# A four-layer conditioned trunk in fp32: first loads reordered, operands laid out at multiples of 256 bytes, one sub-layer's end split into halves

## The chip, the cores and the metric

The kernel runs on one core of one Trainium2 chip. The time is device microseconds of one execution; the figure for the kernel before is the median of three runs.

## The reference, cut to what matters

There are 512 tokens of width 1024 and four layers. Each layer has a token mixer (layer 0 a Conformer convolution module, 1 HGRN2, 2 mLSTM, 3 stick-breaking attention) and then a causal gated convolutional FFN of inner width 2816. A vector c modulates each of the eight sub-layers.

```
m = silu(c) @ ada_w[i] + ada_b[i]          # 6 x 1024: shift, scale, gate, twice
h = x * (1 + scale) + shift
x = LayerNorm(alpha * x + (1 + gate) * f(h))
# f of layer 0:
u = glu(h @ w_pw1 + b_pw1);  u = causal_dwconv(u, width 31)
f = silu(layer_norm(u)) @ w_pw2 + b_pw2
```

## The kernel before, in words

All arithmetic is in fp32. A large matrix product is done in three products of float32r operands: each operand is split into a high part (a cast on ScalarE, ACT) and a low part (a subtraction on VectorE, DVE), and TensorE (PE) adds high·high, high·low and low·high in PSUM. Weights stream from HBM once, in units of 128 x 1024 (512 KB). `unit` (L231) loads one into a `raw` buffer (three of them) of the pool `wp`, multiplies it by the gate row where it belongs to an output projection (L242), and `parts` (L247) makes `wh` (L252) and `wl` (L254).

An input projection (`up_mm`, L277) has the weights as the stationary operand and the activations `hh`, `hl` of the pool `xp` as the moving one. An output projection (`down`, L332; `mm` at L345, matmul at L351) has the activations stationary and the weights moving: for each pair of 128 inner rows `kp`, for each block of 128 tokens `t`, six matmuls of 512 columns. `head` makes `down` go over the first pairs for tokens 0 to 255 first and then for tokens 256 to 511; `tail` (3) does the last three pairs token block by token block, so that each can be finished early; the last two of these pairs have their `wh`, `wl` in `spare` tiles of the stage's own pool.

SBUF tiles lie one behind another in pools, at multiples of 32 bytes. By the addresses of the program, `wp` and `xp` (raw, wh, wl, hh, hl, X) lie 192 bytes past a multiple of 256, the FFN's stage pool (the activations `gr..h`, `gr..l` and the spare weights) 64 bytes past one, HGRN's activations 96 or 224 bytes, those of the mLSTM's output projection and of the attention's 64 bytes, and the operands of the mLSTM's value product (`mn`) at 0. In the output projections of HGRN's values (`p_hv`), the attention's values (`p_sv`) and the Conformer (`p_pw`, L351) both operands are at 192.

The modulation is a product with one vector, done on DVE: `ada_unit` (L203) loads 512 KB of ada_w and multiplies and sums it against silu(c) laid out on all partitions (`sbc`), which gives one of 48 columns of a layer. `fill` slips such units between the units of an input projection; `flush` does what is left up to a given column. Columns 0 to 15 are needed for the first h, 16 to 23 for the gate of the mixer, 24 to 39 for the FFN's h.

All loads go out on SyncE's (SP's) queue, in order: a load that waits for a free buffer holds up those behind it. The order of instructions on each engine is worked out by a scheduler at build time, from priorities (the order of the code, weights earlier) and estimated times; then each engine is in order.

The start (`first_h`, L525): loads of the identity, c broadcast to 128 partitions, the layer's parameters, four tiles of X, and then, for each of eight blocks k, two ada units, transposes of X, hf (ACT), hh, hl, and the matmuls of the first four pw1 units.

The Conformer (L627): for each of eight channel blocks j, two pw1 units (with one and two ada units after them, L661 and L662), GLU into `upad` (L667), a spill to DRAM (`ud`, L670) and four loads back with a shift (`R`, L672), 56 convolution matmuls (`pc`, L681), the remaining taps on DVE, transposes to token-major and statistics (L653 to L657). Then LayerNorm of four token blocks (L696), transposes back (L703), SiLU (L705), the split into high and low parts (`ring`, L325 and L326), the gate (`gate_rows`, L433) and `down` with pw2.

Of the kernel before, what the change touches and what calls it, by code (L numbers as in the profile page):

```python
# [10 lines left out]
F32 = mybir.dt.float32  # L11
# [5 lines left out]
P = 128  # L17
# [31 lines left out]
HEAD = 3  # L49

# [19 lines left out]
def pack(inp):  # L70
# [3 lines left out]
    o["c"] = a["c"].reshape(1, D)  # L74
# [65 lines left out]

class Trunk:
    def __init__(self, ctx, tc, ins, out):
# [15 lines left out]
        self.mhalf = self.const.tile([P, 8], F32, name="mhalf")  # L158
# [3 lines left out]
        nc.sync.dma_start(out=cb, in_=ins["c"].broadcast_to([P, D]))  # L162
# [21 lines left out]
    def begin_layer(self, i):  # L184
# [5 lines left out]
        ab = self.sp.tile([P, 48], F32, tag="adab", name=f"adab{i}")  # L190
# [3 lines left out]
        ac = self.sp.tile([P, 48], F32, tag="adac", name=f"adac{i}")  # L194
# [286 lines left out]
    def mod_cols(self, i, which, prev):  # L481
# [10 lines left out]
        GB = self.sp.tile([P, 2 * KD], F32, tag="GB", name=f"GB{i}_{which}")  # L492
# [32 lines left out]
    def first_h(self, i, w=None, us=(), name=None):  # L525
# [5 lines left out]
        with tc.tile_pool(name="start", bufs=1, side="right", reuse_waits="tile") as st:  # L531
# [19 lines left out]
    def sub_end(self, ep, i, which, nxt, bias=None, gate=None, due=True):  # L551
# [22 lines left out]
        def evict(h, t, ps, partial=False):  # L574
# [7 lines left out]
            if h == 0:  # L582
                st[t] = self.sp.tile([P, 2, 6], F32, tag="st", bufs=4, name=f"st_{name}_{t}")
# [22 lines left out]
    def rstd(self, st, name):  # L606
        nc = self.nc
        mv = self.sp.tile([P, 4], F32, tag="mv", bufs=4, name=f"mv_{name}")
# [18 lines left out]
    def conformer(self, nxt):  # L627
# [9 lines left out]
        with tc.tile_pool(name="cf", bufs=1, reuse_waits="tile") as op, ExitStack() as es, \  # L637
                tc.tile_pool(name="cd", bufs=1, space=bass.MemoryType.DRAM) as dr:
# [4 lines left out]
            cf = es.enter_context(tc.tile_pool(name="cg", bufs=1, reuse_waits="tile"))  # L643
# [47 lines left out]
            self.flush(i, 40)  # L691
# [689 lines left out]
```

## Time and profile before

| | us |
|---|---|
| median of 3 runs (2715.63 to 2717.45) | 2715.64 |
| the profiled execution | 2719.89 |
| its span | 2718.1 |
| PE, DVE, ACT busy in it | 2620.6, 1991.0, 1192.1 |

A busy PE is not PE at its peak: matmuls overlap, and the mean duration of one says less than the distance from one start to the next. Where a window of the timeline is full of one kind of matmul, its length divided by their number gives that distance; the count in a window takes in the matmuls that reach in from outside, which is 1 to 2 of them at 0.39 us each. In the trace a plain fp32 matmul stands as two.

### The profile page before, as it was taken

Reading aid. Unit: us, or ns where it says so; the run is one execution under the profiler, and the core shown is the slowest. Engines: PE = TensorE matmul, PEld = TensorE weight load, DVE = VectorE, ACT = ScalarE, POOL = GpSimd, SP = SyncE. Lnnn points to the kernel's source line nnn. Section 1 sums busy time; section 2 is a strip of 40 time slices with the busy share of each in tenths; the row PEclk is TensorE's granted clock in tenths of the full one; section 3 lists DMA queues with packets and bytes.
Section 4 is the critical chain, followed back from the end, with each engine's and each line's share of the span. In section 5 each row is a group of like instructions: output and inputs, shape, how many; then the busy total and the mean of one; then the engine's idle time right before and its main releaser. Section 6 shows DMA issues by size and latency. Waiting matters only on the chain.

```text
span 2718.1 us, 33772 instructions
## 1 busy us (share of the span) xinstructions
PE 2620.6 (96%) x13012; PEld 2099.0 (77%) x13012; DVE 1991.0 (73%) x3051; ACT 1192.1 (44%) x1750; POOL 43.3 (2%) x80
## 2 busy tenths in 40 slices
PE   7979999999998999999999999999999999999998
PEld 5537888887876788888887778888887776888886
DVE  7558997775677799666766777898676577766676
ACT  3124433334774443334555543543434454543332
POOL 0000000000000000000000000000000000000000
PEclk9989999999998999999999999999999999999999
DMA  8843874232221386223222223675323311323232
GB/s 318 242 115 129 299 246 155 97 115 90 86 67 51 114 300 229 93 97 107 87 90 73 86 78 116 211 266 167 101 93 98 96 55 47 101 94 116 93 97 74
DMA packets 109529, 352.66 MB, mean 130 GB/s; under 512 B 12088, under 2 KB 22328, under 8 KB 109368
## 3 DMA queue, kind: packets, MB, share of 16 engines
q1 hardware_dynamic: 109368, 350.50, 39.2%
q8 instruction: 102, 1.67, 0.2%
q14 instruction: 59, 0.48, 0.1%
HBM read 341.96 MB, written 8.50 MB: 129 GB/s over the span
## 4 chain that ended last, share of the span: by engine, by line
PE 81%; DVE 8%; ACT 5%; DMA 3%; issue 2%; POOL 1%; SPq 0%; POOLq 0%; DVEq 0%; ACTq 0%
PE p_f L282 35%; PE p_d L351 16%; PE p_mup L282 6%; PE p_mdn L351 3%; PE p_hqf L282 2%; PE p_sqk L282 2%; PE p_pw L282 2%; PE p_hv L351 1%; PE p_sv L351 1%; PE p_pw L351 1%; DMA ada<-in_ada_dram 1%; PE ms L981 1%; ACT hf L515 1%; PE p_hg L282 1%; DMA r_swo<-in_swo_dram 1%
## 5 line engine op out<-in xcount | busy, mean ns | idle before, releaser
L282 PE MATMUL p_f<-hl,wh_f 128*128 128x512 f32 (+1 forms) x1504 | 565.4, 376 | 1.2 <-DVE hl L522 1.2
L282 PE MATMUL p_f<-hh,wl_f 128*128 128x512 f32 (+1 forms) x1504 | 564.8, 376 | 0.0
L282 PE MATMUL p_f<-hh,wh_f 128*128 128x512 f32 (+1 forms) x1504 | 564.1, 376 | 0.0
L252 ACT CAST wh_f<-r_f 128x1024 fp32r<-128x1024 f32 x176 | 185.0, 1052 | 340.8 <-PE p_f L282 308.3
L282 PEld LDWEIGHTS p_f<-hl,wh_f 128*128 128x128 f32 x1504 | 283.1, 188 | 53.0 <-DVE hl L522 1.6
L282 PEld LDWEIGHTS p_f<-hh,wh_f 128*128 128x128 f32 x1504 | 282.6, 188 | 52.2 <-ACT hh L521 0.9
L282 PEld LDWEIGHTS p_f<-hh,wl_f 128*128 128x128 f32 x1504 | 283.0, 188 | 51.0 <-issue 0.2
L254 DVE TENSOR_TENSOR wl_f<-r_f,wh_f 128x1024 fp32r<-128x1024 f32 x176 | 214.9, 1223 | 136.3 <-ACT wh_f L252 135.8
L208 DVE CUSTOM_DVE_ANT_0 ada<-ada,sbc,adab 128x1024 f32<-128x1024 f32 x192 | 243.4, 1278 | 8.3 <-DMA ada<-in_ada_dram 8.3
L1312 DVE SCALAR_TENSOR_TENSOR cv<-p_f,par,cv 128x511 f32<-128x511 f32 (+1 forms) x176 | 131.1, 745 | 1.4
L1312 DVE SCALAR_TENSOR_TENSOR cg<-p_f,par,cg 128x511 f32<-128x511 f32 (+1 forms) x176 | 131.1, 745 | 1.3
L242 DVE TENSOR_TENSOR r_d<-r_d,gate 128x1024 f32<-128x1024 f32 x88 | 107.5, 1222 | 27.7 <-DMA r_d<-in_fdn_dram 26.7
L1322 ACT ACTIVATE cg<-cg 128x512 f32<-128x512 f32 x88 | 55.4, 629 | 162.2 <-DVE cg L1312 162.2
L254 DVE TENSOR_TENSOR wl_d<-r_d,wh_d 128x1024 fp32r<-128x1024 f32 x88 | 107.4, 1221 | 11.3 <-ACT wh_d L252 11.3
L282 PE MATMUL p_mup<-hh,wh_mup 128*128 128x512 f32 (+1 forms) x280 | 108.4, 387 | 0.9 <-ACT hf L515 0.9
L282 PE MATMUL p_mup<-hh,wl_mup 128*128 128x512 f32 (+1 forms) x280 | 107.1, 382 | 0.0
L282 PE MATMUL p_mup<-hl,wh_mup 128*128 128x512 f32 (+1 forms) x280 | 106.6, 381 | 0.0
L252 ACT CAST wh_d<-r_d 128x1024 fp32r<-128x1024 f32 x88 | 92.3, 1048 | 20.0 <-PE p_f L282 16.0
L624 ACT ACTIVATE X<-X,mv 128x512 f32<-128x512 f32 x56 | 43.1, 810 | 82.0 <-DVE mv L612 82.0
L1310 ACT ACTIVATE cg<-p_f,par 128x512 f32<-128x512 f32 x88 | 68.1, 774 | 13.8 <-PE p_f L282 13.8
L351 PE MATMUL p_d<-wl_d,gr0h 128*128 128x512 f32 x176 | 69.6, 396 | 0.0
L351 PE MATMUL p_d<-wl_d,gr2h 128*128 128x512 f32 x176 | 69.6, 396 | 0.0
(469 smaller groups left out, 5619.5 us busy)
## 6 DMA issues: line engine op xcount, KB each, us to landing
ada<-in_ada_dram SPq DMA_DIRECT2D x192, 512.0 KB, 4.8
r_f<-in_fup_dram SPq DMA_DIRECT2D x176, 512.0 KB, 3.7
r_d<-in_fdn_dram SPq DMA_DIRECT2D x88, 512.0 KB, 3.3
r_mup<-in_mup_dram SPq DMA_DIRECT2D x32, 512.0 KB, 3.3
r_pw<-in_pw_dram SPq DMA_DIRECT2D x24, 512.0 KB, 6.9
r_hqf<-in_hqf_dram SPq DMA_DIRECT2D x16, 512.0 KB, 3.3
r_mdn<-in_mdn_dram SPq DMA_DIRECT2D x16, 512.0 KB, 3.3
r_sqk<-in_sqk_dram SPq DMA_DIRECT2D x16, 512.0 KB, 3.6
```

The source lines that it names most:

```text
L208: nc.vector.tensor_tensor_reduce(out=raw, in0=raw, in1=self.sbc, scale=1.0, scalar=ab[:, j:j + 1], op0=ALU.mult, op1=ALU.add, accum_out=ac ...
L242: nc.vector.tensor_tensor(out=r, in0=r, in1=gr, op=ALU.mult)
L252: nc.scalar.copy(hi, raw)
L254: nc.vector.tensor_tensor(out=lo, in0=raw, in1=hi.bitcast(F32), op=ALU.subtract)
L282: self.nc.tensor.matmul(ps[:, c0:c1], a, b[:, k, c0:c1], start=(n == 0), stop=(n == 3 * KD - 1))
L351: self.nc.tensor.matmul(bank, l[:, ts_], r, start=(kp == first and a == n == 0), stop=(kp == last and a == 1 and n == 2))
L515: nc.scalar.activation(out=hf[:, j, :], in_=ps[:, j * P:(j + 1) * P], func=AF.Identity, scale=G[:, k:k + 1], bias=B[:, k:k + 1])
L624: nc.scalar.activation(out=o[:, hs], in_=x[:, hs], func=AF.Identity, scale=mv[:, 2:3], bias=mv[:, 3:4])
L981: nc.tensor.matmul(ps[:, :n], a[:, c + sb * P:c + (sb + 1) * P], b[:, c + sb * P:c + T], start=(q == 0 and k == 0), stop=(q == 3 and k == 2))
L1310: nc.scalar.activation(out=o, in_=ps, func=AF.Identity, scale=w[2], bias=par[:, C_CONVB + m:C_CONVB + m + 1])
L1312: nc.vector.scalar_tensor_tensor(out=o[:, s:], in0=ps[:, :T - s], scalar=w[2 - s], in1=o[:, s:], op0=ALU.mult, op1=ALU.add)
L1322: nc.scalar.activation(out=cg, in_=cg, func=AF.Silu)
```

## The change

- All pools but three small ones round each tile up to a multiple of 256 bytes (class `Lines`, method `pool`). Small tiles (st, mv, GB, adab, adac, ones, mhalf, and some of HGRN's and mLSTM's) move to pools of their own (`few`, `sm`, `hs`, `mk`) and to one tile at the right edge, sized so that all other tiles start at multiples of 256 bytes.
- c comes from the host already laid out on 128 rows. The order of the first loads becomes c, parameters, two ada units, identity, X. 32 matmuls of ones (into a transpose bank, read by nothing) stand ahead of the first transposes.
- In the Conformer, two ada units instead of three per channel block; the gate is made ahead of the LayerNorm; LayerNorm, transposes, SiLU and the split go in two halves of 256 tokens, the cast of every second block on DVE; the last eight ada units follow the halves; `down` gets head = 3.

```diff
@@ constants
+LINE = 256
+BUSY = 32
@@ pack
-    o["c"] = a["c"].reshape(1, D)
+    o["c"] = np.tile(a["c"].reshape(1, D), (P, 1))
@@ new
+class Lines:
+    def __init__(self, pool):
+        self.pool = pool
+
+    def tile(self, shape, dtype, **kw):
+        n = int(np.prod(shape[1:]))
+        w = LINE // 4
+        if n % w == 0:
+            return self.pool.tile(shape, dtype, **kw)
+        t = self.pool.tile([shape[0], (n + w - 1) // w * w], dtype, **kw)[:, 0:n]
...
@@ Trunk.__init__
-        self.const = E(tc.tile_pool(name="const", bufs=1))
-        self.wp = E(tc.tile_pool(name="wp", bufs=2))
-        self.xp = E(tc.tile_pool(name="xp", bufs=1))
-        self.sp = E(tc.tile_pool(name="sp", bufs=2))
-        self.ps = E(tc.tile_pool(name="ps", bufs=1, space=PSUM))
+        few = E(tc.tile_pool(name="few", bufs=1))
+        few.tile([P, 16], F32, name="edge_l")
+        self.edge = E(tc.tile_pool(name="edge", bufs=1, side="right")).tile([P, 56], F32, name="edge_r")
+        self.const = E(self.pool(name="const", bufs=1))
+        self.wp = E(self.pool(name="wp", bufs=2))
+        self.xp = E(self.pool(name="xp", bufs=1))
+        self.sp = E(self.pool(name="sp", bufs=2))
+        self.sm = E(tc.tile_pool(name="sm", bufs=2))
+        self.ps = E(self.pool(name="ps", bufs=1, space=PSUM))
...
-        nc.sync.dma_start(out=self.ident, in_=ins["ident"])
-        self.ones = self.const.tile([P, 1], F32, name="ones")
+        self.ones = few.tile([P, 1], F32, name="ones")
...
-        nc.sync.dma_start(out=cb, in_=ins["c"].broadcast_to([P, D]))
+        nc.sync.dma_start(out=cb, in_=ins["c"])
+    @contextmanager
+    def pool(self, **kw):
+        with self.tc.tile_pool(**kw) as p:
+            yield p if "space" in kw else Lines(p)
     def load_x(self):
+        self.nc.sync.dma_start(out=self.ident, in_=self.ins["ident"])
         for t in range(NT):
@@ first_h
+        nc.vector.tensor_copy(self.hh[:, KD - 1, :], self.ones.broadcast_to([P, T]))
+        ps = self.trbank("busy")
+        for n in range(BUSY):
+            nc.tensor.matmul(ps, self.onesr, self.hh[:, KD - 1, :], start=True, stop=True)
...
             hl = []
+            self.ada_unit(st, 8)
+            self.ada_unit(st, 8)
+            self.load_x()
             for u in us:
                 self.pre[u] = self.bank(f"p_{name}_{u}")
             for k in range(KD):
-                self.ada_unit(st, 8)
-                self.ada_unit(st, 8)
+                if k:
+                    self.ada_unit(st, 8)
+                    self.ada_unit(st, 8)
@@ conformer
-                pg = self.up(ins["pw1"], KD + j, "pw1", fills=2)
+                pg = self.up(ins["pw1"], KD + j, "pw1", fills=1)
...
-            self.flush(i, 40)
+            self.flush(i, 24)
             self.apool = None
+            gate = self.gate_rows(op, i, 0)
             es.close()
...
-            for t in range(NT):
-                mv = self.rstd(st[t], f"cf{t}")
-                self.normalise(tm[:, t, :], tm[:, t, :], mv)
-            us = []
-            for j in range(KD):
-                ps = self.trbank(f"cb{j}")
-                for t in range(NT):
-                    nc.tensor.transpose(ps[:, t * P:(t + 1) * P], tm[:, t, j * P:(j + 1) * P], self.ident)
-                v = cf.tile([P, T], F32, tag="us", bufs=3, name=f"cs{j}")
-                nc.scalar.activation(out=v, in_=ps, func=AF.Silu, scale=lng(j), bias=lnb(j))
-                us.append(v)
+            ah, al = ([cf.tile([P, T], F32R, name=f"cu{z}{j}") for j in range(KD)] for z in "hl")
+            for s in range(2):
+                for t in (2 * s, 2 * s + 1):
+                    mv = self.rstd(st[t], f"cf{t}")
+                    self.normalise(tm[:, t, :], tm[:, t, :], mv)
+                hs = slice(2 * s * P, 2 * (s + 1) * P)
+                for j in range(KD):
+                    ps = self.trbank(f"cb{j}_{s}")
+                    for t in range(2):
+                        nc.tensor.transpose(ps[:, t * P:(t + 1) * P], tm[:, 2 * s + t, j * P:(j + 1) * P], self.ident)
+                    lo = cf.tile([P, 2 * P], F32, tag="us", bufs=4, name=f"cs{j}_{s}")
+                    nc.scalar.activation(out=lo, in_=ps[:, 0:2 * P], func=AF.Silu, scale=lng(j), bias=lnb(j))
+                    if j % 2:
+                        nc.vector.tensor_copy(ah[j][:, hs], lo)
+                    else:
+                        nc.scalar.copy(ah[j][:, hs], lo)
+                    nc.vector.tensor_tensor(out=al[j][:, hs], in0=lo, in1=ah[j][:, hs].bitcast(F32), op=ALU.subtract)
...
-            gate, evict = self.sub_end(cf, i, 0, nxt, bias)
-            act = self.ring(cf, us, "cu", keep=True)
-            self.down(ins["pw2"], KD, act, "pw2", 2, evict, tail=TAIL, gate=gate,
-                      spare=lambda tag, nm: cf.tile([P, D], F32R, tag="tw", bufs=4, name=nm))
+            self.flush(i, 40, cf, 4)
+            gate, evict = self.sub_end(cf, i, 0, nxt, bias, gate=gate)
+            self.down(ins["pw2"], KD, lambda k, h: (ah[k], al[k]), "pw2", 2, evict, head=HEAD, tail=TAIL, gate=gate,
+                      spare=lambda tag, nm: cf.tile([P, D], F32R, tag="araw", bufs=4, name=nm))
@@ trunk_kernel
         if n == 0:
-            k.load_x()
             if (i, w) == (0, 0):
```

The same wrapping of pools is made in the other sub-layers (`hgrn`, `mlstm`, `stick`, `ffn`), without other edits there.

## Rows read from the trace of the kernel before

**Rows 1.** The page, busy time of each engine: busy us, share of the span, instructions.
```profile
PE 2620.6 (96%) x13012; PEld 2099.0 (77%) x13012; DVE 1991.0 (73%) x3051; ACT 1192.1 (44%) x1750; POOL 43.3 (2%) x80
```

**Rows 2.** Busy time by stretch; last columns granted clock, DMA share, GB/s.
```profile
core 0: us, PE busy (x) PEld busy (x) DVE busy (x) ACT busy (x) POOL busy (x), PEclk, DMA share, GB/s
...
10.00:15.00 5.00, 1.49 (x5) 0.58 (x4) 1.62 (x3) 0.00 (x0) 0.00 (x0) 1.00 1.02 412
...
35.00:40.00 5.00, 5.00 (x25) 3.97 (x24) 5.00 (x9) 3.32 (x5) 0.00 (x0) 1.00 1.03 408
...
50.00:90.00 40.00, 40.00 (x214) 28.70 (x216) 28.75 (x48) 5.75 (x8) 0.00 (x0) 1.00 0.97 288
...
160.00:180.00 20.00, 12.85 (x100) 3.79 (x92) 10.83 (x27) 1.17 (x2) 0.00 (x0) 0.83 0.73 201
180.00:200.00 20.00, 12.12 (x73) 6.77 (x66) 7.89 (x25) 11.47 (x17) 2.61 (x4) 0.67 0.00 0
200.00:220.00 20.00, 16.73 (x63) 12.46 (x62) 17.66 (x18) 9.30 (x13) 0.00 (x0) 0.90 0.32 106
```

**Rows 3.** PE alone in three steady stretches: p_sv, p_d, p_f in that order.
```profile
2092.00:2128.00 36.00, 36.00 (x161) 1.00 0.40 121
1180.00:1280.00 100.00, 100.00 (x432) 1.00 0.32 106
1840.00:1920.00 80.00, 80.00 (x355) 1.00 0.44 146
```

**Rows 4.** PE's timeline, the tail of one FFN down-projection: start us, duration us.
```profile
1279.45 0.40 PE L351 MATMUL p_d<-wh_d,gr1h 128*128 128x512 f32 x1
...
1280.84 0.39 PE L351 MATMUL p_d<-wh_d,gr1h 128*128 128x512 f32 x1
...
1282.20 0.39 PE L351 MATMUL p_d<-wh_d,gr1h 128*128 128x512 f32 x1
```

**Rows 5.** PE's timeline, mLSTM value product, six matmuls apart.
```profile
1499.68 0.39 PE L1121 MATMUL mn<-wh_mv,pl 128*128 128x512 f32 x1
...
1501.04 0.39 PE L1121 MATMUL mn<-wh_mv,pl 128*128 128x512 f32 x1
```

**Rows 6.** Costliest groups: count, busy us, mean ns of one, idle before.
```profile
L351 PE MATMUL p_d<-wl_d,gr0h 128*128 128x512 f32 x176 | 69.6, 396 | 0.0
L208 DVE CUSTOM_DVE_ANT_0 ada<-ada,sbc,adab 128x1024 f32<-128x1024 f32 x192 | 243.4, 1278 | 8.3 <-DMA ada<-in_ada_dram 8.3
L705 ACT ACTIVATE cs<-cb,cpar 128x512 f32<-128x512 f32 x8 | 5.8, 790 | 0.0
L325 ACT CAST cuh<-cs 128x512 fp32r<-128x512 f32 x8 | 4.6, 637 | 0.0
L326 DVE TENSOR_TENSOR cul<-cs,cuh 128x512 fp32r<-128x512 f32 x8 | 5.2, 688 | 6.8 <-ACT cuh L325 6.8
```

**Rows 7.** Timeline of the head: conditioning row, last X tile, first ada, last step.
```profile
6.18 1.06 ACT L163 ACTIVATE sbc<-cb 128x1024 f32<-128x1024 f32 x1 [4.17 <-DMA cb<-in_c_dram]
...
11.99 0.69 PE L540 MATMUL tr_first<-ident,X 128*128 128x128 f32 x2 [0.60 <-DMA X<-in_x_dram]
...
13.38 1.28 DVE L208 CUSTOM_DVE_ANT_0 ada<-ada,sbc,adab 128x1024 f32<-128x1024 f32 x1 [6.33 <-DMA ada<-in_ada_dram]
...
44.75 0.78 ACT L542 ACTIVATE hf_first<-tr_first,adac 128x512 f32<-128x512 f32 x1 [1.76 <-DVE adac L208]
```

**Rows 8.** SP's timeline at the last convolution: two ada loads, then the spill.
```profile
160.29 1.75 SPq L207 DMA_DIRECT2D ada<-in_ada_dram  x2
162.09 0.43 SPq L670 DMA_DIRECT2D ud<-upad  x1
```

**Rows 9.** Chain of waits from the last pw1 unit to pw2: start us, us, what.
```profile
155.94 0.75 DVE upad L667
...
162.09 5.06 DMA ud<-upad
...
168.54 7.26 DMA R<-ud
...
175.94 8.32 PE pc L681 x56
...
192.18 1.28 ACT L705
...
203.88 1.15 DVE r_pw L242
...
206.14 0.96 PE p_pw L351 x3
```

More of the change, by code (lines that the diff above doesn't have):

```diff
@@ L491, in mod_cols @@
         b = self.par[pi][:, C_PB + pw * KD:C_PB + (pw + 1) * KD]
-        GB = self.sp.tile([P, 2 * KD], F32, tag="GB", name=f"GB{i}_{which}")
+        GB = self.sm.tile([P, 2 * KD], F32, tag="GB", name=f"GB{i}_{which}")
         nc.vector.tensor_tensor(out=GB[:, :KD], in0=g, in1=sc, op=ALU.mult)
@@ L530, in first_h @@
         self.new_h("first")
-        with tc.tile_pool(name="start", bufs=1, side="right", reuse_waits="tile") as st:
+        nc.vector.tensor_copy(self.hh[:, KD - 1, :], self.ones.broadcast_to([P, T]))
+        ps = self.trbank("busy")
+        for n in range(BUSY):
+            nc.tensor.matmul(ps, self.onesr, self.hh[:, KD - 1, :], start=True, stop=True)
+        with self.pool(name="start", bufs=1, side="right", reuse_waits="tile") as st:
             hl = []
+            self.ada_unit(st, 8)
+            self.ada_unit(st, 8)
+            self.load_x()
             for u in us:
@@ L636, in conformer @@
         nd = CONV_W - CONV_PE
-        with tc.tile_pool(name="cf", bufs=1, reuse_waits="tile") as op, ExitStack() as es, \
-                tc.tile_pool(name="cd", bufs=1, space=bass.MemoryType.DRAM) as dr:
+        with self.pool(name="cf", bufs=1, reuse_waits="tile") as op, ExitStack() as es, \
+                self.pool(name="cd", bufs=1, space=bass.MemoryType.DRAM) as dr:
             par = op.tile([P, 288], F32, name="cpar")
@@ L642, in conformer @@
             st = [op.tile([P, KD, 6], F32, name=f"cst{t}") for t in range(NT)]
-            cf = es.enter_context(tc.tile_pool(name="cg", bufs=1, reuse_waits="tile"))
+            cf = es.enter_context(self.pool(name="cg", bufs=1, reuse_waits="tile"))
             m4 = cf.tile([P, 32], F32, name="m4")
@@ L930, in hgrn @@
             vs.close()
-            late["p"] = es.enter_context(tc.tile_pool(name="hw", bufs=1, side="right", reuse_waits="tile"))
+            late["p"] = es.enter_context(self.pool(name="hw", bufs=1, side="right", reuse_waits="tile"))
             self.psum(mm="345601", tr="27")
@@ L1145, in mlstm @@
                         nc.vector.tensor_tensor(out=xc[m], in0=xc[m], in1=sz, op=ALU.mult)
-            with tc.tile_pool(name="mb", bufs=1, reuse_waits="tile") as bp:
+            with self.pool(name="mb", bufs=1, reuse_waits="tile") as bp:
                 self.psum(mm="012345", tr="67")
@@ L1156, in stick @@
         HD = 64
-        with tc.tile_pool(name="so", bufs=1, reuse_waits="tile") as op, ExitStack() as es:
+        with self.pool(name="so", bufs=1, reuse_waits="tile") as op, ExitStack() as es:
             so = []
-            kp = es.enter_context(tc.tile_pool(name="sk", bufs=1, reuse_waits="tile"))
+            kp = es.enter_context(self.pool(name="sk", bufs=1, reuse_waits="tile"))
             v = [kp.tile([P, D], F32, name=f"sv{t}") for t in range(NT)]
@@ L1291, in stick @@
             es.close()
-            late["p"] = es.enter_context(tc.tile_pool(name="sf", bufs=1, reuse_waits="tile"))
+            late["p"] = es.enter_context(self.pool(name="sf", bufs=1, reuse_waits="tile"))
             self.psum(mm="234501", tr="67")
@@ L1301, in ffn @@
         up_w, dn_w = self.ins[f"fup{i}"], self.ins[f"fdn{i}"]
-        with tc.tile_pool(name=f"g{i}", bufs=1, reuse_waits="tile") as gp:
+        with self.pool(name=f"g{i}", bufs=1, reuse_waits="tile") as gp:
             gs = [gp.tile([P, T], F32, name=f"g{i}_{j}") for j in range(NF)]
@@ L1351, in trunk_kernel @@
             else:
-                with tc.tile_pool(name="start", bufs=1, reuse_waits="tile") as st:
+                k.load_x()
+                with k.pool(name="start", bufs=1, reuse_waits="tile") as st:
                     k.flush(i, 48, st, 8)
```

51 lines of the change are left out of this document (28 added, 23 removed).

## The prediction

> **What bounds the kernel now.** I read the page first, then busy time by stretch, then the distance between matmuls inside steady stretches, and last the timeline and the chain of waits where stretches are not steady. PE is busy for 2620.6 of 2718.1 us [rows 1], so the end is set by PE: a gain comes either from closing PE's idle stretches, or from making the matmuls themselves follow closer. The reader should see two things. First, nearly all idleness that this change touches lies in the first 210 us. In the head DMA is saturated at 408 to 412 GB/s and, later on, DVE is busy 5.00 of 5.00 us; from 160 to 200 us PE is busy only 12.85 and 12.12 of 20 us, and its granted clock falls to 0.83 and 0.67 [rows 2]. Second, matmuls of the same 512 columns do not follow at the same distance. Taking 1.7 off each count for those that reach in, p_sv has 36 us / 159.3 = 226 ns, p_f 80 / 353.3 = 226 ns, but the FFN's output projection p_d 100 / 430.3 = 232.4 ns, all at full clock [rows 3].
>
> **Part 1: operands at multiples of 256 bytes.** p_sv and p_d come from the same line and loop, so the form of the loop is not the reason. What differs is where the two operands start: in p_sv (and p_f) both are 192 past a multiple of 256, in p_d the moving weights are at 192 and the stationary activations at 64. The tail of one p_d settles it. Up to 1280.84 the weights are in wp: six matmuls take 1280.84 - 1279.45 = 1.39 us, 232 ns each. From 1280.84 on they are the spare tiles of the FFN's own pool, at 64 like the activations: the next six take 1282.20 - 1280.84 = 1.36 us, 227 ns each [rows 4]. So the rest of the division by 256 must be equal for the two operands; its value does not matter, since the mLSTM value product, with both at 0, also has 1.36 us for six [rows 5]. After the change all are at 0, so I expect 226.7 ns everywhere, a gain of 5.7 ns for each matmul that is mismatched now and none for the others.
>
> How many: p_d is 12 groups of 176 [rows 6], 2112, less 192 with spare weights (two pairs of 24 matmuls in each layer), 1920. By the same loop the mLSTM's output projection has 384 less 48, 336. 2256 x 5.7 ns = 12.9 us, in stretches that PE fills without a gap, so all of it counts. HGRN's and the attention's output projections have some 310 more (1.8 us), but are interleaved with waits, of which I expect nearly nothing. The first four pw1 units are mismatched too, under the DVE-bound head: nothing. I take **13 us**, with ends 10 (the tails, where matmuls wait for evictions, not counted) and 14.7 (all counted).
>
> DVE and ACT: their durations come out of the same trace at mixed positions and I cost the change at nothing there; PE hides them in any case. The small pools cost no instruction. No row shows a large load into a tile at a multiple of 256; if it were quicker by a twentieth in the 70 us that are limited by DMA (5 to 40 us, and 50 to 90 with a DMA share of 0.97 [rows 2]), that would be 3.5 us. I take none and keep it for the low end.
>
> **Part 2: the head.** Before, the first ada product starts at 13.38 us, after X has landed (last tile's transposes 11.99), and the last hf at 44.75, 31.4 us later [rows 7]; DVE fills that stretch. Two of the 16 ada units, 1.28 us each [rows 6], now come ahead of X, while DVE sits idle: 2.5 us off the chain. X itself lands about 2.5 us later for them, but what follows step 0 needs DVE, which is now ahead by that much. c laid out may let sbc start sooner than 6.18 [rows 7], and so the two ada; it moves nothing behind X by more than the 1 us or so that its load shrinks. The bytes are the same and DMA is saturated, so the last ada lands hardly sooner: this caps the gain. The 32 matmuls on ones need DVE's copy first and start near 2 us; at full clock distance they are 7.3 us, at half clock (1.2 of 2.4 GHz) 14.5, so they end between 9 and 17 us, and X is due at about 13. PE is in order, so in the worst case the first transposes wait 3 us for them and the gain is gone; with the clock risen on the way they cost nothing. I take **2.5 us**, ends 0 and 4.5.
>
> **Part 3: two ada units per channel block, not three.** Eight units leave the convolution stage: 8 x 1.28 = 10.2 us of DVE, 4.2 MB of DMA. PE is full early in it (40.00 of 40 us from 50 to 90 [rows 2]), so I count only what shows at its end. upad of the last block is ready at 156.7, but its spill goes out at 162.09 [rows 9], because SP stands before two ada loads that are issued from 160.29 for want of a free buffer [rows 8]. With two units per block the four buffers hold two blocks' worth, and the spill goes out near 157: 5 us. The four loads of R (7.26 us [rows 9]) have one 512 KB load less ahead of them: 1.3 us. The last convolution (8.32 us) starts at 175.94 after an idle stretch, and part of it runs at half clock [rows 2, 9]; with the wait gone it should lose some 2 us less. Late next is PE's own work: the convolution before it. **9 us**, ends 4 and 13 (the DMA time of all eight).
>
> **Part 4: halves, early gate, head = 3.** From the end of the last convolution (184.3) to pw2's first matmul (206.14) is 21.9 us, in which SiLU and cast of eight blocks run one after another on ACT from 192.18, and only then the gate, the gate product (203.88) and the weights' cast follow [rows 9]. Now the gate exists before, and its product and both weight parts go into DVE's and ACT's idle time. SiLU of 512 columns takes 0.790 us, the cast 0.637, the low part 0.688 [rows 6]; for 256 I estimate 0.57, 0.40 and 0.42 from these, between one half and the whole. pw2 can start when two blocks of the first half are split: table load 1.28, two SiLU, a cast, a low part, about 3.2 us after 192.2, near 196: 10 us sooner. ACT then brings two blocks in 1.6 us, PE needs 12 x 0.227 = 2.7 us for them, so PE sets the pace. Given back: 16 transposes of the second half now stand inside pw2 (16 x 0.11 us, 1.8; an estimate at half the distance of a 512-column matmul; the half-clock pair in [rows 7] has 0.69 us for two), and DVE, busy 17.66 of 20 us from 200 on [rows 2], has the eight ada units and half the casts to do, of which I let 2.2 us come through. **6 us**, ends -5 (the eight units' 10.2 us stand wholly in front of pw2's weights or low parts) and 10.
>
> **The sum.** 13 + 2.5 + 9 + 6 = 30.5 us, against the profiled execution's 2719.89: 2689.4. The median of the runs is 4.25 us below that execution, so **2685 us**.
>
> **Rivals.** (A) The new order gives nothing: DVE in 185 to 240 us, with ada units ahead of low parts, takes back what parts 2 to 4 bring. For it: 17.66 of 20 us busy. Against: DVE has only 7.89 of 20 us to do from 180 to 200 [rows 2]. Only part 1 is left: 2715.6 - 13 = 2703 us. (B) The change doesn't do what it says on PE: the 232 ns come from something else that the spare tiles share. Against it stand p_sv with wp weights at 226 and mn [rows 3, 5]. Parts 2 to 4 alone: 2698 us. (C) Position 0 brings matmuls nearer to the bare 512 columns at 2.4 GHz, 213.3 ns. 13.3 ns on p_f (4 x 44 x 24 = 4224) and p_d (2112) is 84 us more: about 2601. Against it: mn at 0 follows at 227 like the others [rows 5]. The Trainium skill (TensorE: Matmul & The Clock Gate, Back-to-back issue gap) gives N/2.4 + 2.5 ns for an isolated warm gap, 216 ns for 512 columns; by it these two groups would have 68 us to lose, and a time near 2617. The trace disagrees at every position that it has. (D) Slower: new pool sizes shift which old tile a new one lies on, and at each of the eight sub-layer boundaries a first load waits for a late reader. One landing as in the chain (5.06 us [rows 9]) at each is 40.5 us against 30.5: 2725 us; it decides from 3.8 us per boundary on. Against: first weights come from wp, which outlives the stages.
>
> **How the numbers follow.** Forecast 0.75, A 0.12, B 0.05, C 0.03, D 0.03, what I don't see 0.02. Adding the ends: 10 + 0 + 4 - 5 = 9 us gained gives 2706; 14.7 + 4.5 + 13 + 10 + 3.5 = 45.7 gives 2670. That range takes in A and B and leaves out C and D and little more. About 0.2% (5.4 us) is what a measurement can tell from no change. Faster: 0.75 + 0.12 + 0.05 + 0.03, less 0.02 for mishaps inside them, 0.93; same 0.03; slower 0.04.
>
> **What would show it.** Part 1: a window of p_d holds 442 to 443 matmuls in 100 us, not 432, and the four FFN down-projections shorten by some 2.7 us each; at 432, part 1 is wrong. p_f unchanged at 355 in 80 us; more means C. Head: the last hf near 42 us instead of 44.75; later than 44.75 means that the matmuls on ones or X's later landing count. Part 3: the last spill right behind upad, the last convolution at full clock and ending near 175. Part 4: pw2's first matmul 10 to 12 us after that convolution's end instead of 21.9, then no gap; a gap with DVE at ada units (L208) is A. PE idle at starts of later sub-layers that was not there is D. A time above 2706 makes the sum wrong.

## The result and the profile after

The changed kernel takes **2687.18 us** (median; 2683.66 to 2688.68) against 2715.64: ratio 0.9889, 95% interval 0.9874 to 0.9905. The forecast was 2685, with 2670 to 2706 as its range. The profiled execution took 2686.62 us with a span of 2684.8, 33.3 less than that of before. The sum came out; its terms did so unequally.

PE's busy time on the page, which answers to [rows 1]:

```profile
PE 2603.4 (97%) x13044; PEld 2095.9 (78%) x13044; DVE 1992.3 (74%) x3068; ACT 1193.2 (44%) x1758; POOL 43.8 (2%) x80
```

Busy time by stretch, with the columns of [rows 2] and in its stretches, but for 50 to 90 us:

```profile
10.00:15.00 5.00, 2.33 (x11) 1.05 (x9) 0.49 (x2) 0.35 (x1) 0.00 (x0) 1.00 1.03 420
35.00:40.00 5.00, 5.00 (x25) 3.95 (x24) 5.00 (x9) 3.24 (x5) 0.00 (x0) 1.00 0.91 362
160.00:180.00 20.00, 14.36 (x114) 3.89 (x106) 10.25 (x15) 4.31 (x5) 0.00 (x0) 0.93 0.35 98
180.00:200.00 20.00, 15.97 (x66) 11.04 (x67) 17.11 (x49) 14.63 (x29) 3.31 (x4) 0.68 0.68 237
200.00:220.00 20.00, 20.00 (x90) 16.54 (x90) 19.66 (x27) 7.56 (x9) 0.00 (x0) 1.00 0.41 134
```

In 35 to 40 us nothing moved: PE and DVE are both full, as before. From 180 us on PE has 3.9 and 3.3 us more work in 20; DVE goes from 7.89 to 17.11 and from 17.66 to 19.66 of 20, which matters below.

PE alone in p_sv, p_d and p_f, answering to [rows 3]:

```profile
2062.00:2098.00 36.00, 36.00 (x160) 1.00 0.40 125
1160.00:1260.00 100.00, 100.00 (x443) 1.00 0.33 108
1800.00:1880.00 80.00, 80.00 (x355) 1.00 0.48 158
```

p_d went from 432 to 443 matmuls in 100 us; p_sv and p_f are where they were.

Two timelines of the head, DVE's and ACT's, answering to [rows 7] (start, duration, what; in brackets the idle time before and what ended it):

```profile
7.92 1.28 DVE L238 CUSTOM_DVE_ANT_0 ada<-ada,sbc,adab 128x1024 f32<-128x1024 f32 x1 [2.70 <-DMA ada<-in_ada_dram]
...
16.11 0.69 DVE L583 TENSOR_TENSOR hl_first<-hf_first,hh_first 128x512 fp32r<-128x512 f32 x1 [5.62 <-ACT hh_first L582]
```

```profile
4.41 1.06 ACT L187 ACTIVATE sbc<-cb 128x1024 f32<-128x1024 f32 x1 [2.40 <-DMA cb<-in_c_dram]
...
44.66 0.78 ACT L581 ACTIVATE hf_first<-tr_first,adac 128x512 f32<-128x512 f32 x1 [1.76 <-DVE adac L238]
```

And PE's timeline of the same stretch, the last X tile's first two transposes and the next four:

```profile
14.28 0.44 PE L579 MATMUL tr_first<-ident,X 128*128 128x128 f32 x2 [0.80 <-DMA X<-in_x_dram]
15.48 1.12 PE L579 MATMUL tr_first<-ident,X 128*128 128x128 f32 x4 [0.76 <-ACT hf_first L581]
```

After the matmuls on ones a pair of transposes takes 0.44 us, not 0.69 as in [rows 7]; but by 15.48 four take 1.12, as long as in the trace of before (1.11 us at 16.87): PE is at half speed again (granted clock 0.51 in 15 to 20 us), and of what the ones brought nothing is left. The clock column says nothing of this stretch in the trace of before: it reads 1.00 from 10 to 25 us there, although the transposes are as slow. The first ada product starts 5.5 us sooner, then DVE idles 5.62 us until X has come; the last hf starts at 44.66 instead of 44.75.

SP's queue at the last convolution, answering to [rows 8]:

```profile
151.20 0.34 SPq L709 DMA_DIRECT2D ud<-upad  x1
...
157.72 17.84 SPq L267 DMA_DIRECT2D r_pw<-in_pw_dram  x3
```

The spill goes out right behind upad. The last line is three issues in one: pw2's third weight unit, which goes out at once, and the fourth and fifth. What SP now stands at is the fourth, which finds no buffer and goes out at 174.05.

The chain of waits through the tail, answering to [rows 9] (start, us, what):

```profile
150.42 0.75 DVE upad L706
...
158.73 7.78 PE pc L720 x56
...
168.68 1.14 PE gb L475 x2
...
174.05 3.31 DMA r_pw<-in_pw_dram
...
177.45 1.23 DVE r_pw L272
...
179.82 0.61 DVE cv L728
...
189.45 0.85 PE p_pw L381 x2
```

Two things on it were put there by the change: gb, the early gate's matmul, which stands on PE ahead of the last convolution, and that fourth weight unit, whose gate product (r_pw) and low part stand on DVE ahead of the last cv. That convolution ends at 175.95, and its cv starts 3.9 us later.

By stages, from PE's records, in us (the first three rows are starts: of the last convolution matmul, of the first matmul of pw2, of the first p_f; the others are lengths):

```
                      before   after   difference
last convolution       183.6   175.4     -8.2
first pw2 matmul       206.1   189.1    -17.0
first p_f (Conformer)  254.8   239.5    -15.3
four FFN p_d           499.5   488.9    -10.7
HGRN                   302.8   299.7     -3.1
mLSTM                  413.8   410.0     -3.8   (mdn -1.8)
attention              256.1   255.8     -0.3
```

### The profile page after: what moved, and what is told of

Its sections match the earlier page's. It is cut to its first block, busy times and chain, and to the rows that moved or that the text cites. A ratio compares the mean times of both kernels' runs of the same rounds, so it can differ in the third digit from the quotient of the medians.

```text
span 2684.8 us, 33858 instructions
## 1 busy us (share of the span) xinstructions
PE 2603.4 (97%) x13044; PEld 2095.9 (78%) x13044; DVE 1992.3 (74%) x3068; ACT 1193.2 (44%) x1758; POOL 43.8 (2%) x80
## 4 chain that ended last, share of the span: by engine, by line
PE 83%; DVE 8%; ACT 5%; DMA 2%; issue 2%; POOL 1%; SPq 0%; POOLq 0%; DVEq 0%; ACTq 0%
PE p_f L312 35%; PE p_d L381 16%; PE p_mup L312 6%; PE p_mdn L381 3%; PE p_pw L312 3%; PE p_hqf L312 2%; PE p_sqk L312 2%; PE pc L720 1%; PE p_hv L381 1%; PE p_sv L381 1%; PE p_hg L312 1%; PE ms L1029 1%; ACT hf L545 1%; PE tr L540 1%; PE mn L1168 1%
```

## The experiments

Each ratio is to runs of the kernel before on the same chip (their medians were 2718.0 to 2718.7 us there). The same three points of the Conformer for all, each from one profiled execution:

```
                 ratio   95% interval      last conv.  pw2     p_f
after            0.9889  0.9874 to 0.9905   175.4     189.1   239.5
e_align_only     0.9947  0.9935 to 0.9960   181.8     204.9   252.3
e_order_only     0.9937  0.9925 to 0.9949   173.7     187.3   237.6
e_equal          0.9894  0.9879 to 0.9909   173.3     187.1   237.4
e_head_old       0.9905  0.9890 to 0.9920   175.1     188.8   239.3
e_head_late      0.9904  0.9890 to 0.9919   179.3     192.9   243.1
e_no_halves      0.9904  0.9887 to 0.9920   173.9     190.9   241.6
e_late_gate      0.9916  0.9901 to 0.9931   171.9     196.7   244.9
e_fills3         0.9942  0.9929 to 0.9955   189.1     202.7   255.0
e_best           0.9897  0.9882 to 0.9912   173.4     184.1   242.7
e_best_fill      0.9910  0.9896 to 0.9924   171.6     182.3   242.9
e_best_all       0.9910  0.9897 to 0.9924   174.2     184.9   244.8
```

**Placement and order apart.** e_align_only takes the new pools and Lines into the kernel before and leaves first_h, conformer, load_x and c as they were. e_order_only is the changed kernel with one constant changed:

```
-LINE = 256
+LINE = 4
```

> The kernel before with the placement of the tiles alone changed (every large tile at a multiple of 256 bytes, small ones in pools of their own); loads, convolution stage and its tail as before. Theory: what the later stages gained comes from equal starts of the two matmul operands alone, so this keeps all of it, -18 us (FFN output projections -11, the three later mixers -7): about 2697, p_d 442 matmuls in 100 us, and the first p_f starts at 254 to 255 as before. Rival 1: the later stages are shorter because of the new order (other buffers, other due times), the time is 2715 and p_d stays at 432. Rival 2: placement also makes DMA or DVE quicker and so part of the Conformer's 15 us: below 2692.

> The changed kernel without the rounding of tile sizes (LINE = 4): order, halves and early gate as in it, but 2592 of the fp32r matmuls have their two operands 128 bytes apart in the remainder by 256, the others have equal remainders. Theory A (remainders by 256 have to be equal): p_d at 432 in 100 us, the whole some 15 us quicker than before, about 2700. Theory B (a remainder by 128, 64 or less is enough): p_d at 442, as the changed kernel, 2687. Rival: the order alone gives nothing without the placement, 2715.

Measured: 13.6 us gained (medians) by placement alone, 15.7 by order alone. Together 29.3; the changed kernel's 28.5 agrees within the intervals, so the two simply add. (The 18 us expected of placement had counted all that the later mixers gained: in the trace of e_align_only the mLSTM is 2.3 us shorter, but HGRN and the attention are 0.2 and 0.3 longer.) p_d in 100 us, first in e_align_only, then in e_order_only:

```profile
1175.00:1275.00 100.00, 100.00 (x443) 1.00 0.33 107
```

```profile
1165.00:1265.00 100.00, 100.00 (x433) 1.00 0.33 106
```

In e_order_only p_d's operands are 128 bytes apart, by the addresses of the program, and it still has 433. So theory A holds, theory B is out: a remainder by 128 or less is not enough.

**Equal or a multiple?** e_equal moves every pool by 32 bytes, so that all operands start at 32:

```
-        few.tile([P, 16], F32, name="edge_l")
+        few.tile([P, 24], F32, name="edge_l")
-        self.edge = ....tile([P, 56], F32, name="edge_r")
+        self.edge = ....tile([P, 48], F32, name="edge_r")
```

> The changed kernel with every pool moved by 32 bytes: all matmul operands start 32 past a multiple of 256, so they are equal to each other but no multiple. Theory (only equality counts): as the changed kernel, 2687, p_d 442 matmuls in 100 us. Rival (a multiple of 256 itself counts, for PE or for DMA, DVE and ACT): 5 to 18 us slower, 2692 to 2705; if DMA is the one that gains, the head's last hf comes later than 44.65 us.

```profile
1160.00:1260.00 100.00, 100.00 (x443) 1.00 0.34 110
```

443 and the changed kernel's time: being a multiple of 256 is worth nothing, being equal is. e_probe measures it by itself:

```
SERIES = [(0, 0), (0, 64), (64, 64), (0, 128), ...]     # bytes: stationary, moving
for n in range(36):
    so, mo = s // 4 + 128 * (n % 6), m // 4 + 512 * (n // 3 % 2)
    nc.tensor.matmul(b, S[:, so:so + 128], M[:, mo:mo + 512], ...)
```

> Only loads, fp32r matmuls, one DVE and one ACT operation; nothing of the model is computed. 30 series of 36 matmuls of 512 columns with a new 128-column weight each; series m.._sA_mB has its stationary operand A and its moving operand B bytes past a multiple of 256. Theory (equal remainders by 256): 227 ns from start to start for (0,0), (64,64), (128,128), (192,192), (32,32), (0,256), and 232 ns or more for every unequal pair, by an amount that depends on the difference alone. Rival 1 (remainder by 64): (0,64), (0,128), (0,192) at 227, only (0,32), (0,16), (0,8), (0,4) slower. Rival 2 (the moving operand's own start counts): (64,0) at 227 and (0,64) at 232. 24 loads of 512 KB into tiles at 0, 192, 0, 64 past a multiple of 256: no difference in GB/s between the four groups if placement doesn't bear on DMA; 2 to 3 per cent quicker at 0 if it is what quickened the changed kernel's head.

Six stretches of its PE timeline, each 37 matmuls: the last of the series ahead and one series. A single matmul at the end lasts 0.39, so the distance is (duration - 0.39) / 36.

```profile
61.33 8.74 PE L46 MATMUL m_s_m<-M,S 128*128 128x512 f32 x37
...
86.25 8.80 PE L46 MATMUL m_s_m<-M,S 128*128 128x512 f32 x37
...
161.13 8.77 PE L46 MATMUL m_s_m<-M,S 128*128 128x512 f32 x37
...
169.51 8.55 PE L46 MATMUL m_s_m<-M,S 128*128 128x512 f32 x37
...
211.08 8.55 PE L46 MATMUL m_s_m<-M,S 128*128 128x512 f32 x37
...
235.73 8.71 PE L46 MATMUL m_s_m<-M,S 128*128 128x512 f32 x37
```

In this order they are (0,128), (0,192), (0,32), (32,32), (0,256) and (16,16): 231.9, 233.6, 232.8, 226.7, 226.7 and 231.1 ns. From the starts within each series, in ns:

```
equal      (64,64) 226.7  (128,128) 227.1  (192,192) 227.0  (32,32) 226.7  (0,256) 226.7
           (0,0) in three series without loads beside them 227.3 to 227.9
           (256,0) 226.7  (0,0) beside loads, at the start 231.1
+64        (0,64) 229.4, in part beside loads   (192,0) 229.5   (64,128) 228.9
+128       (0,128) 232.1  (128,0) 233.2   (64,192) 233.3   (192,64) 233.3
+192       (0,192) 233.7  (64,0) 233.4    (128,64) 233.3
+32, +96   (0,32) 232.9   (96,192) 233.7
+224       (32,0) 233.3   (224,192) 233.4
off 32     (16,16) 231.1  (4,4) 237.5     (0,16) 231.5   (16,0) 233.3   (0,8) 233.7   (0,4) 237.1
```

(The number in front is how far the moving operand's remainder lies past the stationary one's.) The theory needs one more condition: at equal starts 16 or 4 past a multiple of 32 the price is paid too. And 232 ns or more for every unequal pair was too much: a moving operand 64 past the stationary one costs 229, one 64 short of it (+192) 233. The rivals are out: (0,64) and (64,0) are both slow. The same matmul with the same weight 36 times also has 226.7 ns. The 32 loads of this kernel, eight each into four tiles that start at 0, 192, 0 and 64, ran at 387 to 426 GB/s in steps of 1.25 us, mostly 419, in all four, so these starts made no difference to DMA.

**The head.** e_head_old puts X first again and drops the matmuls on ones:

```
-            self.ada_unit(st, 8)
-            self.ada_unit(st, 8)
             self.load_x()
...
-                if k:
-                    self.ada_unit(st, 8)
-                    self.ada_unit(st, 8)
+                self.ada_unit(st, 8)
+                self.ada_unit(st, 8)
...
-BUSY = 32
+BUSY = 0
```

> The changed kernel with the head of before in two points: X is loaded ahead of the first ada units, each step asks for its two units, and the 32 matmuls on ones are gone; the conditioning row stays laid out. Theory: the head ends when DVE has done its 32 us of ada products and low parts behind one stretch of X's 2 MB, during which it is idle, whichever comes first; so the last hf stays at 44.7 us (44 to 45.2) and the time at 2687. DVE's first ada product then starts near 13 us, later by what it no longer idles between 10.5 and 16.1 us. Rival 1: the order did bring its 2.5 us and something else in the head took them: last hf at 47, 2689 to 2690. Rival 2: the matmuls on ones or X's later landing cost: last hf near 42.5.

DVE's and then ACT's timeline of it:

```profile
13.03 1.28 DVE L238 CUSTOM_DVE_ANT_0 ada<-ada,sbc,adab 128x1024 f32<-128x1024 f32 x1 [7.91 <-DMA ada<-in_ada_dram]
```

```profile
44.38 0.79 ACT L578 ACTIVATE hf_first<-tr_first,adac 128x512 f32<-128x512 f32 x1 [1.76 <-DVE adac L238]
```

The last hf is at 44.38 and the first p_f at 239.3, 0.2 us sooner than in the changed kernel. The head's new order and the matmuls on ones together bring nothing; what each does alone was not run. (Its median is 4.8 us above the changed kernel's, but on its chip the kernel before is 2.3 us slower too, and the intervals of the two ratios overlap. In the profiled execution HGRN and the mLSTM are 6.3 us longer; the last section tells of that.)

e_head_late tries to shorten DVE's chain: the weight splits of three later pw1 units stand behind the last hl.

```
+            self.chain, self.late = (a, b), 3      # last hh copy, last hl; read by up()
...
```

> The changed kernel with one more rule of order: the weight splits of the next three pw1 units (DVE's low parts at 40.3 and 44.5 us among them) stand behind the last hl. Theory (the head ends by DVE's queue): the two low parts, 1.15 us each, leave the chain ahead of the last ada product and hf: last hf at 42.4 instead of 44.65, the first convolution 2.3 us sooner, 2685. Rival: DMA sets the head (the last ada unit lands only then) or PE then waits for the late splits: last hf at 44 to 44.7, or a gap on PE behind the first four pw1 units, 2687 or more.

DVE's and then ACT's timeline near the end of its head:

```profile
41.50 0.69 DVE L583 TENSOR_TENSOR hl_first<-hf_first,hh_first 128x512 fp32r<-128x512 f32 x1 [1.56 <-ACT hh_first L582]
...
46.53 0.69 DVE L583 TENSOR_TENSOR hl_first<-hf_first,hh_first 128x512 fp32r<-128x512 f32 x1 [1.93 <-ACT hh_first L582]
```

```profile
45.07 0.78 ACT L581 ACTIVATE hf_first<-tr_first,adac 128x512 f32<-128x512 f32 x1 [3.60 <-PE tr_first L579]
```

The theory missed. Where the low parts stood, DVE now idles 1.56 and 1.93 us for ACT: they had filled the wait from an ada product over hf and hh to hl. The last hf isn't sooner (45.07): ACT, ahead of it, has idled 3.60 us for PE's transposes, so with DVE's chain shorter PE is what the head waits for. Behind it the three late high parts take 2.94 us on ACT ahead of the first block's sigmoid, and PE waits 1.80 us for that; the whole Conformer is 3.6 us later.

**The tail.** e_no_halves undoes the halves, e_late_gate the early gate:

```
-            for s in range(2):
-                for t in (2 * s, 2 * s + 1):
+            for s in range(1):
+                for t in range(NT):
...
```

> The changed kernel with SiLU, cast and low part in one pass over all four token blocks, as before, the gate still early. Theory (the early gate brings most of part 4): pw2's first matmul comes 3 to 4 us later (two more normalisations and blocks twice as wide), and 2 us come back since no transposes stand between pw2's matmuls: 2688 to 2690. Rival (the halves bring it): 5 to 8 us, 2692 to 2695.

```
-            gate = self.gate_rows(op, i, 0)
...
-            gate, evict = self.sub_end(cf, i, 0, nxt, bias, gate=gate)
+            gate, evict = self.sub_end(cf, i, 0, nxt, bias)
```

> The changed kernel with the gate row built where it was before (at sub_end), the halves kept. Theory (the gate is what pw2 waits for): its two copies, the weights' product with it, cast and low part come behind all SiLU and casts of both halves; pw2's first matmul at 203 to 206 us instead of 189, the transposes no longer stand in pw2 (2 us back), in all 10 to 13 us: 2697 to 2700. Rival (the halves let pw2 start early in any case): below 2692.

Without the halves p_f starts 2.1 us later, without the early gate 5.4. Neither is clear of the changed kernel in the time (the intervals overlap), and p_f alone doesn't show 2 us either: e_equal, the changed kernel at other addresses, has it 2.1 us sooner. What shows it is the stretch from the last convolution to p_f. It is 63.8 to 64.1 us in the five traces with this tail (the changed kernel, e_order_only, e_equal, e_head_old, e_head_late), 67.7 without the halves and 73.0 without the early gate, against 71.2 before. So in this stretch of the changed kernel the early gate brings 8.9 us and the halves 3.6; the halves without the early gate would bring nothing. Of the 10 to 13 us expected without the gate, pw2's later start has 11.1 (24.8 us behind the last convolution instead of 13.7) and 2.2 come back in pw2; only 5.4 are left at p_f because the convolution itself comes 3.5 us sooner. The last two convolutions on PE's timeline, first with the gate late, then in the changed kernel:

```profile
158.56 6.22 PE L720 MATMUL pc<-R,lw 128*32 128x512 f32 x56
...
166.25 6.22 PE L720 MATMUL pc<-R,lw 128*32 128x512 f32 x56
```

```profile
158.66 7.80 PE L720 MATMUL pc<-R,lw 128*32 128x512 f32 x56
...
169.73 6.22 PE L720 MATMUL pc<-R,lw 128*32 128x512 f32 x56
```

The last one starts at 166.25 instead of 169.73; about half of that is the one ahead of it at full speed (6.22 us, in the changed kernel 7.80), the rest the gate's matmul, which is not there. The first half is no merit of the late gate: that convolution takes 6.22 us in e_equal and e_order_only too, and 7.91 in e_head_old. It is most of the scatter of some 2 us in the table's last three columns.

e_fills3 undoes part 3:

```
-                pg = self.up(ins["pw1"], KD + j, "pw1", fills=1)
+                pg = self.up(ins["pw1"], KD + j, "pw1", fills=2)
...
-            self.flush(i, 24)
+            self.flush(i, 40)
```

> The changed kernel with three ada units per channel block again and all units up to 40 flushed ahead of the tail (part 3 undone). Theory (SP stands at ada loads that find no buffer, and so the last spill and the last convolution come late): the last convolution ends 6 to 8 us later than 175.4, at 181 to 184; the tail without the eight units is no shorter, since PE fills it: in all 5 to 8 us, ratio to before 0.991 to 0.992. Rival (part 3 moved DVE work from one busy stretch to another): last convolution late, but pw2 to the first p_f shorter by as much, ratio as the changed kernel, 0.989.

SP's queue and PE's timeline:

```profile
162.20 0.33 SPq L237 DMA_DIRECT2D ada<-in_ada_dram  x1
162.63 1.79 SPq L711 DMA_DIRECT2D R<-ud  x4
...
164.94 0.45 SPq L709 DMA_DIRECT2D ud<-upad  x1
```

```profile
171.19 9.04 PE L720 MATMUL pc<-R,lw 128*32 128x512 f32 x56 [5.10 <-DMA R<-ud]
```

The mechanism is of the expected kind, but one block earlier. SP stands at an ada load from 141 to 162.20 for want of a buffer. Behind it are the four loads of R of the block before the last, for which PE waits 5.10 us; that convolution then takes 9.04 us instead of 7.80, and the last spill comes behind, at 164.94. In the trace of before SP had no such stay at that place: these four loads went out at 145.15. So the size was twice what was expected: the last convolution ends 13.7 us later, and the ratio 0.9942 is that of placement alone. From the last convolution to p_f it is 65.9 us, 5.3 less than before; parts 2 and 4 without part 3 bring nothing in the sum, because that convolution comes 5.4 us later than before.

**Can the tail be better?** e_best moves out of the way what stands on the chain after: the gate's matmuls behind the last transposes, the gate product of the first two weight units behind the first normalisations, the units from the third on, the last ada units and the bias behind the second low part.

```
+            with self.tc.issue_after(self.last):         # last ct transpose
+                gate = self.gate_rows(op, i, 0)
...
+                if name == "pw2" and h == 0:             # ready: 2nd normalisation; split: 2nd low part
+                    es.enter_context(self.tc.issue_after(self.ready if kp < 2 else self.split))
...
+            with self.tc.issue_after(self.split):
+                self.flush(i, 40, cf, 4)
+                gate, evict = self.sub_end(cf, i, 0, nxt, bias, gate=gate)
```

> The changed kernel with another order in the tail alone: the gate's two matmuls behind the last block's transposes on PE, the first two pw2 units' gate product behind the first two normalisations on DVE, the third unit, the last eight ada units and the bias behind the second low part. Theory (PE and DVE work in order, and the early gate and the third unit stand ahead of the last convolution and its cv): last convolution ends at 172 as in the kernel with the late gate, cv no longer at 179.7 but at 172.5, pw2's first matmul at 184 to 185 instead of 189.1: 4 to 5 us, ratio 0.987 to 0.9875. Rival (the weights are then late): pw2's first matmul at 188 or later, ratio 0.989 or more.

pw2's first matmul came at 184.1, as expected, and p_f still 3.2 us later. Busy time by stretch, columns as above, first of the changed kernel, then of e_best:

```profile
205.00:220.00 15.00, 15.00 (x68) 12.43 (x67) 14.66 (x16) 6.03 (x6) 0.00 (x0) 1.00 0.46 144
220.00:225.00 5.00, 5.00 (x24) 4.14 (x23) 5.00 (x11) 0.08 (x1) 0.00 (x0) 1.00 0.28 98
235.00:240.00 5.00, 4.91 (x27) 3.75 (x25) 4.90 (x10) 4.93 (x10) 0.00 (x0) 1.00 0.31 105
```

```profile
205.00:220.00 15.00, 15.00 (x67) 12.17 (x66) 15.00 (x19) 4.12 (x4) 0.00 (x0) 1.00 0.61 202
220.00:225.00 5.00, 3.85 (x18) 2.85 (x17) 5.00 (x9) 0.00 (x0) 0.00 (x0) 1.00 0.22 86
235.00:240.00 5.00, 1.96 (x14) 1.34 (x14) 4.76 (x15) 4.55 (x9) 1.10 (x2) 1.00 0.90 314
```

DVE is full from 205 to 225, and PE, ahead of it, runs out: 1.15 us in 220 to 225, waiting for DVE's first evictions of pw2, and 3.04 in 235 to 240, the longest wait in it ending thus:

```profile
238.99 1.55 PE L543 MATMUL tr<-ident,X 128*128 128x128 f32 x8 [2.99 <-ACT X L666]
```

So in this tail DVE is the second bound, right behind PE: its ada units, low parts, gate products, bias additions and evictions have to be done whenever pw2 starts, and in the order that lets pw2 start sooner ada units stand up to 216 us and the bias additions up to 223, just ahead of the evictions; the first of these comes at 223.15 instead of 221.15.

e_best_fill adds 9 matmuls on ones behind the gate's; e_best_all also asks for each pair of ada units one step earlier in the head.

```
+                ps = self.bank("busy2")
+                for n in range(9):
+                    nc.tensor.matmul(ps, self.onesr, self.hh[:, KD - 1, :], start=True, stop=True)
```

> As the one with the other order in the tail, and 9 matmuls on ones behind the gate's, where PE else idles some 4 us. Theory (PE's clock falls after that idle stretch and makes the transposes and the first ten pw2 matmuls slow): transposes of cb at 0.55 to 0.65 us for four instead of 1.1, first pw2 matmuls at 0.23, 2 to 3 us more, ratio 0.986. Rival (the fill stands in front of the transposes, or the clock falls all the same): no difference to the one without, 0.987 to 0.9875.

```
-                if k:
+                if k < KD - 1:                    # the pair of step k + 1
                     self.ada_unit(st, 8)
-                    self.ada_unit(st, 8)
+                    self.chain = self.ada_unit(st, 8),
+                    self.late = 3
```

> As the one with 9 matmuls on ones, and in the head each pair of ada units is asked for one step earlier, the later pw1 units' low parts behind them. Theory (the head ends by the order in DVE's queue: last ada pair, then hf, hh, hl, with two low parts of later units in between): last hf at 41.5 to 42.5 instead of 44.65, first convolution at 70 instead of 72.5, 2 to 2.5 us more, ratio 0.985. Rival (PE, at half clock in the head, or its later weights set the first convolution): last hf earlier, first convolution not before 72, no difference.

Neither is better. With the 9 matmuls the granted clock was 1.00 in 175 to 180 and 0.82 in 180 to 185, and then fell all the same, to 0.50 in 185 to 190 (e_best without them: 1.00, 0.70, 0.62). In e_best_all the last two hf came early, on ACT's timeline:

```profile
42.20 1.45 ACT L585 ACTIVATE hf_first<-tr_first,adac 128x512 f32<-128x512 f32 x2 [3.25 <-PE tr_first L583]
```

but ACT had idled 3.25 us for PE ahead of them, as in e_head_late, and the first convolution stayed at 73.0 us (72.5 in the changed kernel): the rival held, an earlier hf doesn't move it. No version here is measurably better than the changed kernel.

## Why the prediction was right, and where it wasn't

**Part 1 (13 us): right in mechanism and size.** 13.6 us by the medians of e_align_only; in its trace p_d loses 10.7 and the mLSTM's mdn 1.8 (the prediction had 12.9 for both). Its Conformer is 2.5 us shorter too, which had been put at nothing; that it is placement's isn't shown, since executions with one and the same tail differ by as much as 2 us there. What the prediction could not know is that the rule has a second half (a start off a multiple of 32 costs even if equal) and that the price depends on which operand lies ahead (229 ns at +64, 233 at +192). Rival C is out as the trace of before had it: with both operands at 0, and with one weight for all, the distance is 226.7 to 227.9 ns. The Trainium skill (TensorE: Matmul & The Clock Gate, Back-to-back issue gap) gives 216 ns as the isolated warm gap at 512 columns; no run here shows that for these fp32r matmuls, of which the closest followed at 226.7.

**Part 2 (2.5 us): wrong, nothing came.** The step that failed is "2.5 us off the chain", and in it that what follows step 0 "needs DVE, which is now ahead by that much". Two ada units ahead of X did move into idle time, but X's 2 MB then came later and DVE idled while they did: 5.62 us after the units instead of 6.33 ahead of them. And even a shorter DVE chain would not have paid. The row of 35 to 40 us in [rows 2] has PE at 5.00 of 5.00 beside DVE at 5.00; the prediction read one column of it. e_best_all shows the other: last hf some 1.8 us sooner, first convolution no sooner. (That the first convolution came at 72.5 instead of 74.1 goes with part 3: with three ada units per block, in e_fills3, it is at 74.5.)

**Part 3 (9 us): right in mechanism.** The spill went out at 151.20, behind upad, 10.9 us sooner: 5.4 of that is the ada loads no longer ahead of it, and 5.5 is upad itself, which the prediction had left at 156.7. The last convolution starts 6.2 us sooner and takes 6.22 us instead of 8.28, the "2 us less"; it ends 8.2 us sooner, and 9.9 and 10.3 in e_order_only and e_equal, where the one ahead of it ran at full speed. What kept it from starting as soon as R had landed was PE's own work, the convolution before it, as the prediction said, and gb. But the term isn't one that stands by itself: taken out of the finished change it costs 13.7 us at the same place.

**Part 4 (6 us): 7.1, by other amounts.** From the last convolution to p_f it was 71.2 and is 64.1 us. pw2 starts 13.7 us after that convolution instead of 22.5, 8.8 sooner where 10 were forecast; of the 4.0 put down as given back, 1.7 were (pw2's start to p_f: 48.7, now 50.4): sixteen transposes stand in pw2, and PE has no gap that DVE made. The prediction did not see what the early gate itself delays: its matmul and the fourth weight unit stand ahead of the last convolution and the last cv, in queues that go in order. It did see DVE as the limit (rival A), and A was nearer than 0.12 looks: in e_best pw2 starts 5 us sooner than in the changed kernel, and none of it is left at p_f.

**The sum** of 30.5 us met 28.5. Part 2 brought 2.5 less, part 3 a little less, parts 1 and 4 a little more; that the misses nearly cancel is luck. Conformer 15.3 in the trace (17.2 in e_order_only) where parts 2 to 4 had 17.5. No boundary wait of rival D appeared. HGRN's 3.1 us and 2.0 of the mLSTM's 3.8 in the two profiled executions belong to no part: they are for the most part the scatter that the last section shows.

## What to carry to other kernels

Where matmuls of one shape follow at two distances, look at where their operands start before looking at the loop: stationary and moving operand with the same remainder by 256, at multiples of 32, were 2.4% less per matmul in p_d here (226.7 ns against 232.4). Shortening a chain that runs through one engine brought nothing in this head, where another engine was full in the same row: read all columns of a stretch. And when something is done early, look at what it stands in front of in an in-order queue, and which engine is the next bound: e_best started pw2 5 us sooner and lost all of it.

## What the runs showed that was not expected

The scatter of this kernel is PE's clock in few places. In the changed kernel and in e_head_old every engine has the same instructions in the same order from 65 us on, yet HGRN takes 299.7 and 302.6 us, and the first 500 matmuls of the mLSTM's up projection, with what stands between them, 191.5 and 194.7. PE alone in the latter (busy, granted clock, DMA share, GB/s), first the changed kernel, then e_head_old:

```profile
1460.00:1464.00 4.00, 4.00 (x16) 0.70 0.57 199
1464.00:1468.00 4.00, 4.00 (x19) 1.00 0.06 25
1468.00:1472.00 4.00, 4.00 (x21) 1.00 0.00 0
```

```profile
1460.00:1464.00 4.00, 3.31 (x11) 0.79 0.74 254
1464.00:1468.00 4.00, 4.00 (x13) 0.50 0.42 132
1468.00:1472.00 4.00, 4.00 (x11) 0.50 0.00 0
```

A wait of PE of 2.98 us ends just ahead in both, at 1457.98 and 1460.68; once the clock (at 1.2 of 2.4 GHz) rises after a few matmuls, once after many. In HGRN's projections and the mLSTM's up projection the changed kernel has some 10 matmuls at 0.43 us instead of 0.23, e_head_old some 35, the kernel before some 29. Those 25 more, at 0.2 us each, are 5 of the 6.3 us that e_head_old's two stages are longer; the 19 more of the kernel before are 3.8 us. A difference of 3 us in one stage of one profiled execution is therefore no finding here, unless queues or distances differ.

The two loads of the conditioning row differ too: laid out and first in the queue, SiLU of it starts at 4.41 us, broadcast from one row and behind the identity at 6.18 [rows 7]; which of the two did it was not run, and nothing waited for it.
